# A hybrid decoder trunk on one core: rows of x scaled and transposed instead of multiplied by a diagonal, and squares added on the vector engine before they are summed

## The chip, the cores and the metric

The program runs on one core of a Trainium2 chip. The metric is the time that one execution takes on the device, in microseconds (us). PE is the matrix engine, DVE the vector engine, ACT the scalar engine, POOL the general-purpose engine; SP issues nearly all DMAs. All of them work through their own instructions in order and wait for each other by semaphores.

## The reference, cut to what matters

Two layers, each with a token mixer of four parallel groups (MLA, S5, NSA, gated DeltaNet) and a gated FFN with a short convolution. 256 tokens, 2048 features, FFN width 5632, float32. Around each of the four sub-layers stand an RMS norm before (with shift and scale computed from a conditioning vector c) and one after; three of the mixers' outputs are normalised over their 512 features, and the MLA query and key-value latents over 384 and 256.

```python
def rms_norm(x, g):
    xf = x.astype(jnp.float32)
    y = xf * lax.rsqrt(jnp.mean(xf * xf, axis=-1, keepdims=True) + NORM_EPS)
    return (y * g.astype(jnp.float32)).astype(x.dtype)

q = (rms_norm(cq, q_norm) @ w_uq).reshape(B, S, MLA_HEADS, MLA_NOPE + MLA_ROPE)
kv = (rms_norm(ckv, kv_norm) @ w_ukv).reshape(B, S, MLA_HEADS, MLA_NOPE + MLA_V)

o = jnp.concatenate([rms_norm(o_a, gn_mla), rms_norm(o_b, gn_s5), rms_norm(o_c, gn_nsa), o_d], axis=-1)
return o @ w_out
```

## The kernel before, in words

All large products are streamed: a weight tile of 128x1024 floats comes by DMA into a ring (`raw`, four buffers), ACT casts it to the high half of its mantissa (`wh`, line 366), DVE subtracts to get the low half (`wl`, line 367), and PE makes three products of halves for each pair (`mm3`, `mm` at line 127). The activations stand feature-major in the tile `ht`, in two halves too. A second stream (`rawa`, two buffers) brings the modulation weights `w_ada`; DVE multiplies and adds them into `acc` (lines 410 and 412), a tile now and then between other work.

A sub-layer begins in a **turn**. `post_block` gathers sums of squares while the last products of the sub-layer before come out (lines 575 to 586). `residual` works out the scale of the rows, sets it, and adds the new output to x, in four blocks of 512 features for each half of the tokens (line 616). `pre_norm` then makes `ht`: in steps of two chunks of 128 features (`k2`, eight steps), PE multiplies the chunk of x [128 tokens, 128 features], as the stationary operand, by a diagonal matrix `diag` of the rows' scales. This transposes and scales in one product. ACT applies the modulation's scale and shift from PSUM (line 549), DVE (first step) or ACT (the others) casts the high half (line 551), DVE subtracts the low half (line 552). The first four steps stand ahead of the weight products (`norm_start`), the others among them. The additions to x go in two groups: two blocks right behind the diagonals, two behind the first chunks' operands.

`norm_T` (line 695) normalises over features of a feature-major output: ACT squares (line 702), PE multiplies each 128x128 of squares by a column of ones and accumulates over all of them in one PSUM tile, DVE makes the reciprocal root (`row_rs`, lines 516 and 149 to 155), PE spreads it over the partitions, and DVE multiplies (line 709). It is called five times a layer: for four chunks of 256 columns by S5, MLA and NSA, for three by the MLA queries and for two by the MLA keys and values.

Transposes elsewhere go through `tp` (line 131). The order of each engine's instructions is set by a scheduler while the program is built, from the program order and from priorities: the weight stream stands up to 2500 steps ahead (`BOOST`), the turn ahead of that (`first`), and `after` puts instructions behind a given one.

Of the kernel before, what the change touches and what calls it, by code (L numbers as in the profile page):

```python
# [21 lines left out]
P = 128  # L22
# [21 lines left out]
RSC = -8192.0        # factor that rsqrt_cols leaves on its result  # L44

MBOOST = 300        # the same of the mixers' own weights
BOOST = 2500        # how far ahead of the arithmetic the weight stream is scheduled

# arena map (floats per partition)
A_KVT = 0                           # token-major narrow columns  # L50
A_SIL0 = A_KVT + 1704               # GDN inputs of heads 0, 1
A_GA = A_SIL0 + 1536                # S5, then GDN heads 0, 1, then MLA
A_SIL1 = A_GA + 6160                # S5 tables; GDN inputs of heads 2, 3
A_GB = A_SIL1 + 1536                # S5 tables; GDN heads 2, 3, then NSA
A_OT = A_GB + 7168                  # mixer outputs, feature-major
A_KEEP = A_OT + 4096                # compressed keys and values of the NSA group
NA = A_KEEP + 1024
A_X = A_KVT                         # the residual stream, but for the time of the mixers
A_Z = A_X + 4096                    # output of the mixing block before its norm
A_GP = A_SIL1                       # the output gate of the mixing block  # L60
FIRST = (O_U, O_U + 256, O_GQ)      # columns of the first products
A_TAB = A_SIL1                      # S5 tables, the rotations last
A_ROT = A_TAB + 4608
A_SCR, N_SCR = A_OT + 2048, 3072    # S5 tables being built
A_GPF = A_SCR                       # the output gate of the FFN
AT = [A_ROT + g * 1024 for g in range(4)] + [A_Z + g * 1024 for g in range(5)] + [A_OT, A_OT + 1024]   # the FFN's inner activations
ADA_DVE = (0, 2, 4, 6, 9, 11)       # tiles of a quarter that DVE multiplies
# [6 lines left out]
class Region:  # L74
    """Sequential carving of a range of the arena."""
# [16 lines left out]
class Ker:  # L92
    def __init__(self, ctx, tc, I, out):
# [5 lines left out]
        # operands in two parts of half the mantissa: h^T; then the mixer outputs, or the FFN's activations  # L99
# [410 lines left out]
    def first(self):  # L510
        """Ahead of the weight stream."""
        return self.tc.high_priority(BOOST + 1500)

# [15 lines left out]
    def pre_norm(self, l, which):  # L529
        """Fills h^T, 4 tiles of 4 chunks each; a generator that stops after each quarter of the features."""  # L530
        nc = self.nc
        for k2 in range(KT // 2):
            if k2 in (2, 4, 6):
                yield
# [1193 lines left out]
```

## Time and profile before

| | |
|---|---|
| Time of three runs | 2695.22 us median (2687.34 to 2700.55) |
| Profiled execution | span 2692.3 us from its first to its last instruction; the page gives no time of its own around it |
| Busy | PE 2553.3 us (95%), PE weight loads 2257.8 (84%), DVE 1924.8 (71%), ACT 1260.7 (47%) |
| DMA | 621.43 MB, 231 GB/s in the mean |
| Granted PE clock, mean | 0.978 |

A profile shows for each engine when an instruction was at work and what it waited for before. The stages lie like this: up to about 172 us the start (constants, the first modulation vectors, the first norm), to 560 us the mixers of the first layer, to 625 their output projection, then the first FFN to about 1418, the second layer's mixers from 1440 to 1850, their projection to 1915, and the second FFN to the end. The turns lie at 625 to 641, 1425 to 1440 and 1915 to 1930 us.

### The profile page before, as it was taken

What the parts mean: (1) busy time and instruction counts of PE and PEld (TensorE: products, weight loads), DVE (VectorE), ACT (ScalarE), POOL (GpSimd) and SP (SyncE); (2) the same over time, 40 slices, a digit from 0 to 9 for tenths busy, and PEclk for the clock granted to TensorE, in tenths of its full rate; (3) what the DMA queues carried; (4) which work ended last, traced back from release to release, by engine and by line L of the source; (5) the groups of instructions that cost most, each with busy time, mean ns of one, the idle gap of its engine ahead of it and who ended that gap; (6) DMA issues with size and microseconds to landing.
All of it is one profiled execution on the core that took longest, in us unless ns stands there. A gap on an engine that the chain in (4) does not pass through costs nothing. (4 is left out here: it accounts for less than half of the span.)

```text
span 2692.3 us, 44696 instructions
## 1 busy us (share of the span) xinstructions
PE 2553.3 (95%) x17587; PEld 2257.8 (84%) x17587; DVE 1924.8 (71%) x3036; ACT 1260.7 (47%) x2025; POOL 9.6 (0%) x21
## 2 busy tenths in 40 slices
PE   5899999798999999999998999999899999999998
PEld 2478788687999999988877879888799999998886
DVE  6668888778877777776878888865677655555555
ACT  4244554546545444444545445555544444444443
POOL 0000000000000000000000000000000000000000
PEclk7889999899999999999999999999999999999999
DMA  8986887676888888877776667835588766665554
GB/s 269 298 242 188 259 277 226 202 268 217 274 287 277 283 286 284 293 247 234 232 255 228 189 201 243 267 123 170 180 272 280 224 187 188 183 186 188 188 188 148
DMA packets 325899, 621.43 MB, mean 231 GB/s; under 512 B 45132, under 2 KB 131640, under 8 KB 324152
## 3 DMA queue, kind: packets, MB, share of 16 engines
q1 hardware_dynamic: 317632, 617.36, 71.5%
q8 instruction: 138, 2.26, 0.3%
q10 hardware_dynamic: 8056, 1.21, 0.3%
q14 instruction: 73, 0.60, 0.1%
HBM read 614.26 MB, written 4.23 MB: 230 GB/s over the span
## 5 line engine op out<-in xcount | busy, mean ns | idle before, releaser
L127 PE MATMUL mm<-ht,wh 128*128 128x256 f32 x7232 | 1311.4, 283 | 2.9 <-ACT wh L366 2.9
L366 ACT CAST wh<-raw 128x1024 fp32r<-128x1024 f32 (+1 forms) x740 | 771.2, 1043 | 953.8 <-PE mm L127 751.2
L367 DVE TENSOR_TENSOR wl<-raw,wh 128x1024 fp32r<-128x1024 f32 (+1 forms) x740 | 893.2, 1213 | 346.1 <-ACT wh L366 344.2
L127 PEld LDWEIGHTS mm<-ht,wh 128*128 128x128 f32 x7232 | 1114.1, 189 | 15.2 <-issue 6.8
L127 PE MATMUL mm<-ht,wl 128*128 128x256 f32 x3616 | 1023.9, 283 | 7.9 <-DVE wl L367 7.6
L127 PEld LDWEIGHTS mm<-ht,wl 128*128 128x128 f32 x3616 | 681.7, 189 | 20.2 <-DVE wl L367 12.8
L412 DVE SCALAR_TENSOR_TENSOR acc<-rawa,condc,acc 128x1024 f32<-128x1024 f32 x310 | 397.3, 1282 | 216.5 <-DMA rawa<-in_w_ada_dram 215.0
L127 PE MATMUL mm<-wh,ht 128*128 128x512 f32 (+1 forms) x1600 | 507.4, 395 | 3.4 <-ACT ht L366 2.9
L127 PEld LDWEIGHTS mm<-wh,ht 128*128 128x128 f32 x1600 | 300.9, 189 | 68.0 <-ACT ht L366 3.2
L127 PE MATMUL mm<-wl,ht 128*128 128x512 f32 (+1 forms) x800 | 316.1, 395 | 1.7 <-DVE wl L367 1.7
L127 PE MATMUL mx<-wh,ht 128*128 128x512 f32 x704 | 221.4, 395 | 0.0
L127 PE MATMUL mx<-arena 128*128 128x128 f32 (+8 forms) x1432 | 199.1, 280 | 12.5 <-ACT arena L1417 4.7
L127 PEld LDWEIGHTS mx<-arena 128*128 128x128 f32 (+5 forms) x1432 | 156.0, 170 | 51.4 <-issue 20.2
L127 PEld LDWEIGHTS mm<-wl,ht 128*128 128x128 f32 x800 | 151.6, 190 | 34.0 <-DVE wl L367 3.0
L127 PEld LDWEIGHTS mx<-wh,ht 128*128 128x128 f32 x704 | 132.0, 187 | 32.1
L127 PE MATMUL mx<-wl,ht 128*128 128x512 f32 x352 | 139.3, 396 | 0.9 <-DVE wl L367 0.8
L131 PE MATMUL mx<-ident,arena 128*128 128x128 f32 (+3 forms) x367 | 68.4, 290 | 32.4 <-ACT arena L1280 11.0
L367 DVE TENSOR_TENSOR ht<-arena,ht 128x1024 fp32r<-128x1024 f32 x52 | 63.6, 1223 | 39.4 <-ACT ht L366 39.0
L131 PEld LDWEIGHTS mx<-ident,arena 128*128 128x128 f32 (+3 forms) x367 | 44.4, 148 | 53.7 <-ACT arena L1280 12.7
L1557 DVE SCALAR_TENSOR_TENSOR arena<-mm,v,arena 128x255 f32<-128x255 f32 (+1 forms) x176 | 78.2, 476 | 4.3 <-ACT arena L1555 3.5
L127 PEld LDWEIGHTS mx<-wl,ht 128*128 128x128 f32 x352 | 66.0, 187 | 18.1 <-DVE wl L367 2.1
L366 ACT CAST ht<-arena 128x1024 fp32r<-128x1024 f32 x52 | 54.2, 1050 | 56.5 <-PE mm L127 32.3
(308 smaller groups left out, 1514.1 us busy)
## 6 DMA issues: line engine op xcount, KB each, us to landing
raw<-in_ffn_w_in_dram SPq DMA_DIRECT2D x352, 512.0 KB
rawa<-in_w_ada_dram SPq DMA_DIRECT2D x348, 512.0 KB
raw<-in_ffn_w_out_dram SPq DMA_DIRECT2D x176, 512.0 KB
raw<-in_w_in_dram SPq DMA_DIRECT2D x116, 512.0 KB
raw<-in_w_out_dram SPq DMA_DIRECT2D x64, 512.0 KB
rawm<-in_w_ada_dram SPq DMA_DIRECT2D x28, 512.0 KB
raw<-in_w_in_dram SPq DMA_DIRECT2D x16, 426.0 KB
raw<-in_w_in_dram SPq DMA_DIRECT2D x16, 354.0 KB
```

What stands on the lines that cost most here:

```text
L127: self.nc.tensor.matmul(out, lhsT=lhsT, rhs=rhs, start=start, stop=stop)
L131: self.nc.tensor.transpose(out, in_, self.ident[:k, :k])
L366: self.nc.scalar.copy(hi.bitcast(F32R), src)
L367: self.nc.vector.tensor_sub(lo.bitcast(F32R), src, hi)
L412: self.last_mac = self.nc.vector.scalar_tensor_tensor(acc, w, self.condc[:, kc:kc + 1], acc, op0=ALU.mult, op1=ALU.add)
L1557: nc.vector.scalar_tensor_tensor(c[:, s:], ps[m][:, :256 - s], self.fconv(l, 2 - s, f), c[:, s:], op0=ALU.mult, op1=ALU.add)
```

## The change

The diagonal is gone. `set_scale` leaves the rows' scale as two columns. `pre_norm` copies a quarter of x (512 features, both halves of the tokens) times that scale into a free place of the arena: DVE does so for the first quarter, ACT for the other three. PE then transposes the copies with `tp`. The additions to x now go in three groups: one block behind the scale, one behind the scaled copies of the first quarter, two as before. `norm_T` squares all chunks into one place of 1024 floats, DVE adds the squares down to 256 columns, and PE makes two products with the column of ones instead of two for each chunk. (Comments of the file are left out in the changed kernel; its line numbers differ a little.)

```diff
-        self.diag = t([P, 2, P], F32, "diag")
...
-    def set_diag(self, ss):
+    def set_scale(self, ss):
+
         r = self.rsqrt_cols(ss)
-        for tt in range(2):
-            i = self.nc.vector.tensor_scalar(self.diag[:, tt], self.ident, r[:, tt:tt + 1], 1.0 / RSC,
-                                             op0=ALU.mult, op1=ALU.mult)
-        return i
+        self.rs = self.sm(2, "rs")
+        return self.nc.vector.tensor_scalar(self.rs, r, 1.0 / RSC, None, op0=ALU.mult)
 
     def pre_norm(self, l, which):
         nc = self.nc
+        slots = (AT[0:4] if which else (AT[7], AT[8], AT[4], AT[5]) if l else (AT[9], AT[10]))
         for k2 in range(KT // 2):
             if k2 in (2, 4, 6):
                 yield
+            if k2 % 2 == 0:
+                q = k2 // 2
+                xs = self.reg(slots[q % len(slots)], 1024)(2, 512)
+                for tt in range(2):
+                    src = self.x[:, tt, q * 512:(q + 1) * 512]
+                    if q:
+                        nc.scalar.activation(xs[:, tt], src, AF.Identity, scale=self.rs[:, tt:tt + 1])
+                    else:
+                        i = nc.vector.tensor_scalar(xs[:, tt], src, self.rs[:, tt:tt + 1], None, op0=ALU.mult)
+                if q == 0 and self.add_rest is not None:
+                    self.add_rest[0](i)
             ps = self.mx()
             for i in range(2):
-                k = 2 * k2 + i
+                k = (2 * k2 + i) % 4
                 for tt in range(2):
-                    self.mm(ps[:, i * 256 + tt * P:i * 256 + (tt + 1) * P], self.x[:, tt, k * P:(k + 1) * P],
-                            self.diag[:, tt], True, True)
+                    self.tp(ps[:, i * 256 + tt * P:i * 256 + (tt + 1) * P], xs[:, tt, k * P:(k + 1) * P])
...
-                self.add_rest(i)
+                self.add_rest[1](i)
...
-        d = self.set_diag(t)
+        d = self.set_scale(t)
...
-        add(range(2), d)
-        self.add_rest = lambda i: add(range(2, 4), i)
+        add(range(1), d)
+        self.add_rest = [lambda i: add(range(1, 2), i), lambda i: add(range(2, 4), i)]
...
     def norm_T(self, scr, chunks, banks, n, gains, outs):
         nc = self.nc
+        o = 0
+        for b, w in banks:
+            nc.scalar.activation(scr[:, o:o + w], b, AF.Square)
+            o += w
+        sq = scr[:, 0:256]
+        if o == 1024:
+            nc.vector.tensor_tensor(scr[:, 0:512], scr[:, 0:512], scr[:, 512:1024], op=ALU.add)
+            o = 512
+        for i in range(256, o, 256):
+            nc.vector.tensor_tensor(sq, sq, scr[:, i:i + 256], op=ALU.add)
         ss = self.mx(2)
-        i, m = 0, 2 * len(chunks)
-        for bi, (b, w) in enumerate(banks):
-            sq = scr[:, bi % 2 * 512:bi % 2 * 512 + w]
-            nc.scalar.activation(sq, b, AF.Square)
-            for j in range(w // P):
-                self.mm(ss[:, j % 2:j % 2 + 1], sq[:, j * P:(j + 1) * P], self.ones[:, 0:1], i == 0, i == m - 1)
-                i += 1
+        for j in range(2):
+            self.mm(ss[:, j:j + 1], sq[:, j * P:(j + 1) * P], self.ones[:, 0:1], True, True)
```

The scheduler lays the program out anew. Three places:

PE's order at the turn into the first FFN, before (`mx` are PSUM tiles of one step each, `mm` those of the weight products):

```order
L127 MATMUL mx_5672<-diag,arena 128x128
L127 MATMUL mx_5688<-diag,arena 128x128
L127 MATMUL mx_5672<-diag,arena 128x128 x3
L127 MATMUL mx_5688<-diag,arena 128x128 x3
L127 MATMUL mx_5698<-diag,arena 128x128 x4
L127 MATMUL mx_5708<-diag,arena 128x128 x4
L127 MATMUL mm<-ht,wh 128x256 x2
```

and with the change:

```order
L131 MATMUL mx_5666<-ident,arena 128x128 x4
L131 MATMUL mx_5682<-ident,arena 128x128 x4
L131 MATMUL mx_5694<-ident,arena 128x128
L131 MATMUL mx_5704<-ident,arena 128x128
L127 MATMUL mm<-ht,wh 128x256 x3
L127 MATMUL mm<-ht,wl 128x256
L127 MATMUL mm<-ht,wh 128x256 x2
L127 MATMUL mm<-ht,wl 128x256
L127 MATMUL mm<-ht,wh 128x256
L127 MATMUL mm<-ht,wl 128x256
L127 MATMUL mm<-ht,wh 128x256 x2
L127 MATMUL mm<-ht,wl 128x256
```

Sixteen products stood ahead of the first weight product, ten transposes do now; the other six of the first four steps stand behind twelve weight products.

DVE's order at the same turn, before:

```order
L525 TENSOR_SCALAR diag<-ident,cy 128x128 x2
L616 SCALAR_TENSOR_TENSOR arena<-arena,cy 128x512 x4
L551 CAST ht<-hf 128x256
L552 TENSOR_TENSOR ht<-hf,ht 128x256
L551 CAST ht<-hf 128x256
L552 TENSOR_TENSOR ht<-hf,ht 128x256
L616 SCALAR_TENSOR_TENSOR arena<-arena,cy 128x512 x4
L552 TENSOR_TENSOR ht<-hf,ht 128x512 x2
L367 TENSOR_TENSOR wl<-raw,wh 128x1024 x2
```

and with the change:

```order
L524 TENSOR_SCALAR rs<-cy 128x2
L625 SCALAR_TENSOR_TENSOR arena<-arena,cy 128x512 x2
L542 TENSOR_SCALAR arena<-arena,rs 128x512 x2
L625 SCALAR_TENSOR_TENSOR arena<-arena,cy 128x512 x2
L560 CAST ht<-hf 128x256
L561 TENSOR_TENSOR ht<-hf,ht 128x256
L560 CAST ht<-hf 128x256
L561 TENSOR_TENSOR ht<-hf,ht 128x256
L625 SCALAR_TENSOR_TENSOR arena<-arena,cy 128x512 x4
L561 TENSOR_TENSOR ht<-hf,ht 128x512
L366 TENSOR_TENSOR wl<-raw,wh 128x1024
```

Two scalings stand between the additions of the first and second block, and one subtraction less ahead of the first split of a weight tile (`wl`).

ACT's order there with the change, from the last weight casts before the turn on (before, the two casts were followed by the shifts into `hf` at once):

```order
L365 CAST wh<-raw 128x1024 x2
L540 ACTIVATE arena<-arena,rs 128x512
L558 ACTIVATE hf<-mx_5666,mod 128x256 x2
L558 ACTIVATE hf<-mx_5682,mod 128x256 x2
L540 ACTIVATE arena<-arena,rs 128x512
L560 CAST ht<-hf 128x512
L540 ACTIVATE arena<-arena,rs 128x512
L558 ACTIVATE hf<-mx_5694,mod 128x256 x2
L540 ACTIVATE arena<-arena,rs 128x512
```

The scalings of the second and third quarter (L540) stand between the shifts and casts of the first steps.

In SP's order the loads are the same 1256 in number. Ahead of the 109th load into `raw` stood 98 loads into `rawa`, and 87 do now; ahead of the 115th it is 113 and 111, and from the 121st on to the second layer's mixers the two counts agree again.

## Rows read from the trace of the kernel before

**Rows 1.** The page, part 1: busy us, share of the span, instructions.

```profile
span 2692.3 us, 44696 instructions
PE 2553.3 (95%) x17587; PEld 2257.8 (84%) x17587; DVE 1924.8 (71%) x3036; ACT 1260.7 (47%) x2025; POOL 9.6 (0%) x21
```

**Rows 2.** By stage: length, busy us of PE, PEld, DVE, ACT, POOL, clock, DMA.

```profile
0.00:172.00 172.00, 123.04 (x676) 66.42 (x677) 104.22 (x269) 60.64 (x143) 4.61 (x13) 0.82 0.88 281
172.00:500.00 328.00, 316.72 (x2224) 271.45 (x2223) 275.48 (x546) 155.94 (x308) 0.52 (x1) 1.00 0.76 232
500.00:560.00 60.00, 47.09 (x288) 39.52 (x289) 37.49 (x80) 31.64 (x82) 2.27 (x2) 0.89 0.64 204
...
1440.00:1850.00 410.00, 400.56 (x2832) 348.29 (x2831) 317.53 (x647) 213.21 (x448) 0.52 (x1) 0.99 0.67 209
```

**Rows 3.** Timeline, turn into the first FFN: start, us, instruction, idle before and releaser.

```profile
633.25 0.48 DVE L525 TENSOR_SCALAR diag<-ident,cy 128x128 f32<-128x128 f32 x2
633.65 2.73 DVE L616 SCALAR_TENSOR_TENSOR arena<-arena,cy 128x512 f32<-128x512 f32 x4
...
634.49 6.35 PE L127 MATMUL mx<-diag,arena 128*128 128x128 f32 x32 [9.51 <-issue]
637.00 1.02 ACT L549 ACTIVATE hf<-mx,mod 128x256 f32<-128x256 f32 x2 [6.72 <-PE mx L127]
...
637.93 0.43 DVE L552 TENSOR_TENSOR ht<-hf,ht 128x256 fp32r<-128x256 f32 x1
...
640.60 0.48 PE L127 MATMUL mm<-ht,wh 128*128 128x256 f32 x2
```

**Rows 4.** Groups by line and shape, PE: count, busy us, mean ns, idle before.

```profile
L127 PE MATMUL mx<-diag,arena 128*128 128x128 f32 x256 | 40.2, 318 | 26.2 <-issue 17.9 <-DVE arena L616 7.0 <-DVE diag L525 0.7
...
L127 PE MATMUL mx<-ones,arena 128*128 128x1 f32 x168 | 20.8, 244 | 0.4 <-ACT arena L702 0.3
```

**Rows 5.** Timeline of PE: eight records of diagonal products, eight of transposes.

```profile
643.99 1.05 PE L127 MATMUL mx<-diag,arena 128*128 128x128 f32 x8
...
1633.02 1.05 PE L131 MATMUL mx<-ident,arena 128*128 128x128 f32 x8
```

**Rows 6.** Groups by line and shape, DVE.

```profile
L412 DVE SCALAR_TENSOR_TENSOR acc<-rawa,condc,acc 128x1024 f32<-128x1024 f32 x310 | 397.3, 1282 | 216.5 <-DMA rawa<-in_w_ada_dram 215.0
...
L1339 DVE TENSOR_TENSOR arena<-arena 128x512 f32<-128x512 f32 x64 | 42.0, 682 | 0.1
...
L1180 DVE TENSOR_TENSOR arena<-arena 128x256 f32<-128x256 f32 x48 | 19.5, 421 | 6.5 <-ACT arena L1242 6.0
...
L410 DVE TENSOR_SCALAR acc<-rawa,condc 128x1024 f32<-128x1024 f32 x23 | 17.2, 749 | 4.0 <-DMA rawa<-in_w_ada_dram 4.0
```

**Rows 7.** Busy time and clock around that turn; then PE's timeline near the start.

```profile
634.50:639.80 5.30, 5.30 (x25) 5.30 (x26) 4.01 (x9) 2.04 (x4) 0.00 (x0) 0.50 0.01 3
639.90:643.20 3.30, 3.30 (x31) 3.30 (x30) 3.30 (x6) 2.99 (x6) 0.00 (x0) 1.00 0.00 0
...
31.50:33.50 2.00, 1.82 (x8) 1.57 (x8) 0.85 (x7) 0.67 (x3) 0.00 (x0) 0.50 1.01 369
31.68 1.94 PE L131 MATMUL mx<-ident,arena 128*128 128x128 f32 x8 [2.80 <-DMA arena<-in_s_c_re_dram]
```

**Rows 8.** Timeline, the first layer's S5 norm.

```profile
281.52 0.16 DVE L516 TENSOR_SCALAR rv<-mx 128x2 f32<-128x2 f32 x1 [2.28 <-PE mx L127]
```

**Rows 9.** The chain that ended last, turn into the second FFN: start, us, what.

```profile
1930.95 1.21 DVE ht L552 x2
1932.16 1.15 DVE wl L367
```

**Rows 10.** Timeline, the first layer's MLA norm.

```profile
517.22 0.63 ACT L702 ACTIVATE arena<-arena 128x512 f32<-128x512 f32 x1
...
519.37 1.28 DVE L412 SCALAR_TENSOR_TENSOR acc<-rawa,condc,acc 128x1024 f32<-128x1024 f32 x1 [1.51 <-DMA rawa<-in_w_ada_dram]
520.57 0.15 DVE L516 TENSOR_SCALAR rv<-mx 128x2 f32<-128x2 f32 x1
```

More of the change, by code (lines that the diff above doesn't have):

```diff
@@ L1643, in run @@
         self.new_squares()
-        self.set_diag(self.x_stats())
+        self.set_scale(self.x_stats())
         h = self.pre_norm(0, 0)
```

## The prediction

> **What bounds the kernel now.** I read the page first: PE is busy for 95% of the span, DVE for 71%, so the first question is where PE is not kept fed [rows 1]. Busy time by stage [rows 2] puts the idle time into a few places. In the mixers of both layers PE is busy for 97% and 98% of the stage and DVE for 84% and 77%; over the last 60 us of the first layer's mixers PE falls to 78%. The other holes are the turns, where one sub-layer's output is normalised before the next one can start. There are three; I read the one into the first FFN in the timeline [rows 3]. PE stands still for 9.5 us while DVE computes the rows' scale; then DVE writes the two diagonals, adds two blocks of x, and PE starts its diagonal products at 634.49, although the first weight product comes only at 640.60, behind all 32 records of the first four chunk pairs. Its operand was ready sooner: ACT took the scaled and shifted half at 637.00, DVE cast it and subtracted at 637.93 for 0.43, so by 638.36 the operand was there. PE's own queue holds the first product back by 2.2 us.
>
> **Products against transposes.** The program has 128 products with the diagonal and the trace shows 256 records of them [rows 4]: two records each. Eight such records (four products) take 1.05 us; eight records of a transpose, which are eight transposes, also take 1.05 us [rows 5]. Less the last one's latency (0.27) that is 0.111 us for a record. So a product costs PE 0.222 and a transpose 0.111, and 128 of them give back 14.2 us of PE. A quarter of that belongs to the first norm, which lies in the opening stretch where PE is only 72% busy [rows 2]; I cost it at nothing, since loads cover it there, and at 3.6 us of loss at most if the scaling lengthens that start.
>
> **A turn, step by step** (the first FFN's, times from [rows 3]). The scale is known at 633.25. DVE then writes one tile of two columns instead of two diagonals: about 0.2 instead of 0.4. It adds the first block of x for both halves of the tokens (four take 2.73, so two about 1.4), and now scales both. A 128x512 TENSOR_SCALAR is in no row; it lies between the 128x128, two of which take 0.48 [rows 3], and the 128x1024 of 0.75 [rows 6], in proportion at about 0.47 (bounds 0.24 and 0.75). The first transposes can go at about 635.3, the second half's at 635.7: PE starts 0.8 us later than before. It is at the low level of its clock there; eight transposes in a row at that level take 1.94 us, 0.22 each [rows 7]. The four of the first chunk pair end, with latency, at about 636.8. ACT first scales half of the second block (its add ends at 636.4; a 128x512 pass of ACT takes 0.63 [rows 10], with a scale per row perhaps 0.7), so it takes the chunk at 637.1; cast and subtraction follow as before, and the first operand is there at 638.45. By the new order only ten transposes stand ahead of the first weight product, so that starts at 638.45 and not at 640.60: 2.15 us sooner. Against that, six transposes (0.65) come later among the products, and until the clock rises at 639.8 [rows 7] the products run at half speed (0.7 lost). Net gain 0.8. Chunk pairs five to eight stand among the products: 16 x 0.111 = 1.8 us less. A turn gains 2.6. One rule speaks against this; it stands with the third rival.
>
> What could take that back is the supply. ACT gets six scalings of about 0.7 per norm, 4.2 us, in a stretch in which it also shifts, casts and splits weights; DVE's four late adds and the first weight split stand in the chain of the third turn [rows 9]. There the order changes for the better: one subtraction (0.6) moves behind the first weight split. I take 7 us for three turns. Bounds: 0, if ACT's scalings hold each turn up, and 10.7, if all of the PE time of three norms (three quarters of 14.2) is gained.
>
> **Norms over features.** Ten calls lose 48 products with a column of ones, 96 records of the 168 [rows 4], 0.111 each: 10.7 us of PE. DVE gets six adds of 128x512 at 0.68 and twelve of 128x256 at 0.42 [rows 6]: 9.1 us. PE is the fuller engine in the mixers, so I count some of its time as gained, not all. On the chain of one norm it cuts both ways. In the S5 norm DVE sat idle for 2.28 us until PE had summed [rows 8]; with two adds (1.1) and two products (four records, 0.45) the sums come about 0.7 us sooner. In the MLA norm at the end of the mixers the squares were done at 517.85 but DVE was in a modulation product that had waited 1.51 us for its load; the sums were read at 520.57 [rows 10]. Adds queued behind that product would give the sums 1.6 us later. I take 3 us as the net of all ten calls; bounds are a loss of 9.1 and a gain of 10.7.
>
> **Order.** All of the mixers are laid out anew, SP's loads too: 87 modulation loads instead of 98 stand ahead of the 109th weight load, and they have caught up twelve weight loads later. Each costs DVE 1.28 us [rows 6]. It is work moved, not added: zero, with 11 x 1.28 = 14 us either way as the bound. Everything in the FFNs but the turns keeps its order.
>
> **Sum.** 7 + 3 = 10 us off the profiled execution's 2692.3 us of span. The page gives no time around that span; the median of the runs is 2695.2, 2.9 above it, and I add that: 2682.3 + 2.9 = **2685 us**.
>
> **Rivals.**
> *All PE time is gained.* PE is 97 to 98% busy in the mixers, and after a turn each record is followed by the next. Then 10.7 from the norms and 10.7 from the three turns come off: 2695.2 - 21.4 = 2674 us. Against it: DVE is at 77 to 84% there, and gets 9.1 us more.
> *Slower: DVE's queue at the end of the mixers.* DVE works in order, and it waited 215 us before its modulation products for their loads [rows 6]; every add placed behind such a product waits with it. This decides if PE runs out of weight products there, as it did between 500 and 560 [rows 2]. Price: the eleven modulation products moved towards the end at 1.28 plus the mean wait of 0.7 (215 us over their 310), 21.8 us, and 1.6 us at each of the four late norms, less the turns' 7 and a little from the early mixers, about 5: 16 us more, 2711 us. For it speaks PE's 78%; against it, that the loads moved are missing earlier, and that between the softmax steps the new order has no more of these products than the old one.
> *The clock stays low.* At the first FFN's turn PE stood still for 9.5 us [rows 3], the granted clock was 0.50 (1.2 GHz) while it did diagonal products, and 1.00 (2.4 GHz) from 639.9 [rows 7]. If transposes do not bring it back as those products did, the rise comes later by the time from the first record to the first weight product, 638.45 - 634.49 = 4.0 us, in which half the work is lost: 2.0 a turn, 6 in all, and nearly all of the turns' gain is gone: 2691 us. The eight transposes in rows 7 also ran at 0.50, but only just after a wait, so the trace does not decide. The Trainium skill, TensorE: Matmul & The Clock Gate, Part 4 (PE-mode transpose), says that the full clock "doesn't engage" for transposes; by that rule this rival holds, and no long run of transposes alone in this trace shows it.
> *It does not do what it says.* A transpose costs no less than a product once its scaled copy is counted: 32 passes of ACT and DVE (eight a norm) replace PE time that was never waited for. Then the time stays at 2695. Rows 3 speak against it, since PE's queue is what the first weight product waits for.
>
> **How the numbers follow.** Runs of this kernel lie between 2687 and 2701, so 0.5% (13.5 us) is about what can be told from no change; below 2682 is faster, above 2709 slower. Chances: forecast 0.45 (2677 to 2693), all PE time gained 0.30, low clock 0.10, no effect 0.05, slower 0.10. Faster: the second case and the lower quarter or so of the first, 0.40. Slower: 0.10. The rest, 0.50, is no change. The range runs from 2670, just under the case of all PE time with some favour of the order, to 2704, above no effect by some of the order's 14 us; it leaves out most of the slower case and the tails.
>
> **What would show it.** Right: the first weight product of the first FFN about 3.1 us after PE's first transpose of the turn, where 6.1 lay behind the first diagonal product, ten transposes ahead of it, transposes with one record each, PE's busy time down by some 20 us. Wrong in the turn: ACT's scalings end PE's waits, or the granted clock rises later than 5 us after PE resumes. Wrong in the mixers: PE's share between the MLA norm and the last norm falls below 78%, or DVE's wait for modulation loads grows well past 215 us.

## The result, and the profile after

The changed kernel takes 2709.6 us (median of 6 runs, 2700.2 to 2712.3), the kernel before 2694.0 (6 runs): a ratio of 1.0062, interval 1.0042 to 1.0082. It is **slower by 0.6%**, 15.6 us, where 2685 was forecast and 2704 was the end of the range. Four of the six runs lie at 2709 to 2712 and two at 2700 to 2701; the trace is of one of the four.

The page of the changed kernel, part 1:

```profile
span 2708.2 us, 44327 instructions
PE 2544.3 (94%) x17363; PEld 2238.9 (83%) x17363; DVE 1937.9 (72%) x3058; ACT 1278.5 (47%) x2053; POOL 9.6 (0%) x21
```

Against [rows 1], PE is busy for 9.0 us less, and yet the span grew. The groups of records that the change touches, the transposes before and after and the products with ones after, shrank by more:

```profile
L131 PE MATMUL mx<-ident,arena 128*128 128x128 f32 x334 | 63.3, 294 | 28.2 <-ACT arena L1280 11.0 <-ACT arena L740 8.3 <-DMA arena<-in_s_c_re_dram 2.8
```

```profile
L131 PE MATMUL mx<-ident,arena 128*128 128x128 f32 x462 | 87.6, 308 | 70.9 <-DVE arena L542 27.6 <-ACT arena L754 17.5 <-ACT arena L1294 11.1
L127 PE MATMUL mx<-ones,arena 128*128 128x1 f32 x72 | 9.6, 244 | 3.1 <-DVE amx L742 2.3 <-DVE arena L716 0.7
```

The 128 new transposes take 24.3 us where the diagonal products took 40.2, and the products with ones 9.6 where they took 20.8 [rows 4]. But the mean granted clock fell from 0.978 to 0.969, and at the lower level a record takes longer (eight transposes 1.94 us at 0.50 in [rows 7], 1.05 in [rows 5]).

Busy time by stage (length, then busy us of PE, PEld, DVE, ACT, POOL, clock, DMA share, GB/s) tells where:

```profile
0.00:172.00 172.00, 117.75 (x631) 59.15 (x632) 101.31 (x262) 61.40 (x141) 4.62 (x13) 0.81 0.84 274
172.00:500.00 328.00, 312.53 (x2165) 265.54 (x2163) 272.43 (x535) 159.04 (x304) 0.53 (x1) 0.99 0.74 232
500.00:560.00 60.00, 40.26 (x191) 32.80 (x190) 37.14 (x87) 28.40 (x89) 0.00 (x0) 0.72 0.48 153
```

Against [rows 2], PE falls from 47.1 to 40.3 us between 500 and 560, its clock there from 0.89 to 0.72, and the DMA share from 0.64 to 0.48. A stage cut at fixed times compares different work, though. So the first layer is cut here at three instructions that both kernels have: DVE reads the sums of S5's norm (`rv<-mx`, the first), those of the recurrence's second pair of heads (`rv<-gss`, the third), and reduces the block sums at the first turn (`bt<-bs`). Weight tiles are counted by their splits on DVE:

| stretch, us | before | before, a second trace | after |
|---|---|---|---|
| A: start to S5's sums | 281.5 (42 tiles) | 281.7 | 290.3 (43) |
| B: to the second heads' sums | 105.0 (20) | 107.9 | 116.1 (25) |
| C: to the first turn | 241.9 (45) | 242.4 | 246.8 (39) |
| first turn to second | 800.0 | 799.5 | 794.7 |
| second turn to third | 489.3 | 486.5 | 487.1 |
| third turn to the end | 774.6 | 775.5 | 773.3 |

Two traces of the kernel before differ by 3.6 us at most at these points. The change loses 8.7 + 11.1 + 4.9 = 24.7 us in the first layer up to its first turn and gains 8.8 after it: all of the loss lies in A, B and C (against the second trace, 21.1 are lost there and 5.2 gained after). Of these, B holds five more weight tiles than before, and C six fewer. A weight tile is just under 3 us of PE (in the FFN, 200 splits of the kernel before take 595 us), so B is longer by less than the work that moved into it. C, with some 18 us less to do at the full clock, should be shorter by as much; it is 4.9 longer. Stretch C, before and then after:

```profile
386.50:628.40 241.90, 218.68 (x1349) 181.99 (x1347) 187.41 (x377) 117.72 (x248) 2.27 (x2) 0.97 0.74 241
```

```profile
406.30:653.10 246.80, 209.81 (x1242) 172.70 (x1240) 181.56 (x374) 111.44 (x240) 2.28 (x2) 0.92 0.67 219
```

PE is busy there for 8.9 us less, at a mean granted clock of 0.92 and not 0.97, and stands still for 37.0 us and not 23.2.

The groups of DVE in stretch C, before and then after (busy, mean ns of one, idle time ahead):

```profile
L412 DVE SCALAR_TENSOR_TENSOR acc<-rawa,condc,acc 128x1024 f32<-128x1024 f32 x53 | 67.9, 1281 | 20.4 <-DMA rawa<-in_w_ada_dram 20.2
```

```profile
L411 DVE SCALAR_TENSOR_TENSOR acc<-rawa,condc,acc 128x1024 f32<-128x1024 f32 x51 | 65.4, 1282 | 35.5 <-DMA rawa<-in_w_ada_dram 35.3
```

About as many modulation products as before, but DVE waits 15 us longer for their loads (12.5 longer than in the second trace of before, which has 22.8). Over the whole program this wait is 215.0 and 186.3 us in the two traces of before and 196.6 after, so the sum over a program does not show it. The chain that ended last shows what this looks like, in the changed kernel from 504 us on (start, us, what):

```profile
504.40 1.20 DVE acc L411
...
505.62 4.88 DMA rawa<-in_w_ada_dram
...
510.60 1.30 DVE acc L411
511.92 4.37 DMA rawa<-in_w_ada_dram
516.31 1.29 DVE acc L411
...
517.62 4.35 DMA rawa<-in_w_ada_dram
...
522.06 1.30 DVE acc L411
523.37 4.29 DMA rawa<-in_w_ada_dram
```

A product frees its buffer, the next load into it lands 4.3 us later, and there are two buffers: two products every 5.7 us, with DVE in order and the softmax steps behind them. That is the pace when nothing else lies between. Before, weight tiles lay between: the longest row of modulation products without a split of a weight tile among them has 12 in both traces of before (496.8 to 534.7 in the first), and **23** after (470.0 to 541.3).

The turn into the first FFN, which answers to [rows 3]:

```profile
658.05 0.17 DVE L524 TENSOR_SCALAR rs<-cy 128x2 f32<-128x2 f32 x1
658.12 1.41 DVE L625 SCALAR_TENSOR_TENSOR arena<-arena,cy 128x512 f32<-128x512 f32 x2
659.45 0.87 DVE L542 TENSOR_SCALAR arena<-arena,rs 128x512 f32<-128x512 f32 x2
...
660.08 2.49 PE L131 MATMUL mx<-ident,arena 128*128 128x128 f32 x10 [10.42 <-DVE arena L542]
...
661.65 1.91 ACT L558 ACTIVATE hf<-mx,mod 128x256 f32<-128x256 f32 x4
662.23 0.29 DVE L560 CAST ht<-hf 128x256 fp32r<-128x256 f32 x1 [0.58 <-ACT hf L558]
...
662.57 1.04 PE L127 MATMUL mm<-ht,wh 128*128 128x256 f32 x3
```

The first weight product comes 2.5 us after the first transpose, ten transposes ahead of it, as forecast (6.1 and sixteen products before). From the reduction of the block sums to the 192nd weight record it takes 38.4, 37.8 and 37.7 us at the three turns before, and 35.6, 36.1 and 36.4 after: 2.8, 1.8 and 1.3 gained, 5.9 in all. The granted clock there:

```profile
664.40:664.80 0.40, 0.40 (x4) 0.40 (x3) 0.40 (x1) 0.40 (x2) 0.00 (x0) 0.53 0.00 0
664.80:665.20 0.40, 0.40 (x5) 0.40 (x5) 0.40 (x2) 0.40 (x1) 0.00 (x0) 1.00 0.00 0
```

It reaches 1.00 at 664.8, 4.7 us after PE resumed (5.3 before). And two norms, on DVE: S5's, for [rows 8], then MLA's, for [rows 10]:

```profile
285.38 1.27 DVE L411 SCALAR_TENSOR_TENSOR acc<-rawa,condc,acc 128x1024 f32<-128x1024 f32 x1
286.57 0.69 DVE L713 TENSOR_TENSOR arena<-arena 128x512 f32<-128x512 f32 x1
287.18 1.22 DVE L366 TENSOR_TENSOR wl<-raw,wh 128x1024 fp32r<-128x1024 f32 x1
288.31 0.42 DVE L716 TENSOR_TENSOR arena<-arena 128x256 f32<-128x256 f32 x1
...
290.26 0.16 DVE L515 TENSOR_SCALAR rv<-mx 128x2 f32<-128x2 f32 x1 [1.14 <-PE mx L127]
...
533.42 1.28 DVE L411 SCALAR_TENSOR_TENSOR acc<-rawa,condc,acc 128x1024 f32<-128x1024 f32 x1 [1.62 <-DMA rawa<-in_w_ada_dram]
534.62 0.68 DVE L713 TENSOR_TENSOR arena<-arena 128x512 f32<-128x512 f32 x1
535.23 0.68 DVE L741 TENSOR_REDUCE amx<-mx 128x2 f32<-128x512 f32 x1
535.83 0.42 DVE L716 TENSOR_TENSOR arena<-arena 128x256 f32<-128x256 f32 x1
...
537.00 0.16 DVE L515 TENSOR_SCALAR rv<-mx 128x2 f32<-128x2 f32 x1 [0.68 <-PE mx L127]
```

The adds stand in DVE's queue behind whatever was laid ahead of them: a split of a weight tile between S5's two adds, a modulation product that had waited for its load ahead of MLA's. From the end of the last square to the sums, six norms (S5, MLA, NSA of both layers) took 2.5, 2.7, 2.0, 2.2, 1.8 and 1.8 us before and 4.6, 2.7, 3.2, 5.3, 2.5 and 2.2 after.

### The profile page after: what moved, and what is told of

Read it like the earlier page. It is cut to its first block, busy times and chain, and to the rows that moved or that the text cites. A ratio compares the mean times of both kernels' runs of the same rounds, so it can differ in the third digit from the quotient of the medians.

```text
span 2708.2 us, 44327 instructions
## 1 busy us (share of the span) xinstructions
PE 2544.3 (94%) x17363; PEld 2238.9 (83%) x17363; DVE 1937.9 (72%) x3058; ACT 1278.5 (47%) x2053; POOL 9.6 (0%) x21
## 4 chain that ended last, share of the span: by engine, by line
PE 73%; DMA 11%; DVE 9%; ACT 3%; issue 3%; SPq 0%; ACTq 0%; DVEq 0%
PE mm L127 55%; PE mx L127 16%; DMA rawa<-in_w_ada_dram 9%; DVE wl L366 3%; DVE acc L411 2%; PE mx L131 2%; ACT wh L365 1%; DMA rawm<-in_w_ada_dram 1%; DMA raw<-in_w_in_dram 1%; ACT junk L584 1%; DMA rawm<-in_nsa_w_v_dram 0%; DMA arena<-in_s_c_im_dram 0%; DVE arena L590 0%; ACT arena L1294 0%; DVE arena L1044 0%
## 5 line engine op out<-in xcount | busy, mean ns | idle before, releaser
L411 DVE SCALAR_TENSOR_TENSOR acc<-rawa,condc,acc 128x1024 f32<-128x1024 f32 x310 | 397.3, 1282 | 197.4 <-DMA rawa<-in_w_ada_dram 196.6
L127 PE MATMUL mx<-arena 128*128 128x128 f32 (+8 forms) x1432 | 206.7, 289 | 16.7 <-DVE arena L1044 5.9
L127 PEld LDWEIGHTS mx<-arena 128*128 128x128 f32 (+5 forms) x1432 | 162.6, 177 | 62.0 <-issue 18.9
L131 PE MATMUL mx<-ident,arena 128*128 128x128 f32 (+3 forms) x495 | 92.9, 304 | 76.0 <-DVE arena L542 27.6
L131 PEld LDWEIGHTS mx<-ident,arena 128*128 128x128 f32 (+3 forms) x495 | 63.5, 155 | 100.4 <-issue 33.7
```

Source lines behind the costliest of these rows:

```text
L127: self.nc.tensor.matmul(out, lhsT=lhsT, rhs=rhs, start=start, stop=stop)
L131: self.nc.tensor.transpose(out, in_, self.ident[:k, :k])
L411: self.last_mac = self.nc.vector.scalar_tensor_tensor(acc, w, self.condc[:, kc:kc + 1], acc, op0=ALU.mult, op1=ALU.add)
```

## The experiments

Three theories were tried. *Operations*: the adds, scalings and transposes cost it. *Modulation queue*: DVE stands behind modulation loads at the end of the first mixers. *Order of the weight products*: the scheduler, given other operations, lays the weight products further ahead; they delay the recurrence's steps on PE and are missing at the end (first put as "no filler", then as "ahead of the chain"). Each ratio is to runs of the kernel before on the same chip. A trace is one run and need not lie at the median: e5's took 2708.8 us, e7's 2688.0 and e13's 2693.2, where the medians are 2702.1, 2680.0 and 2699.4.

**Each half alone.** e1 is the changed kernel with the function `norm_T` of before, e2 the kernel before with the new one:

```
 e1, against the change
-        for j in range(2):
-            self.mm(ss[:, j:j + 1], sq[:, j * P:(j + 1) * P], self.ones[:, 0:1], True, True)
...
+            for j in range(w // P):
+                self.mm(ss[:, j % 2:j % 2 + 1], sq[:, j * P:(j + 1) * P], self.ones[:, 0:1], i == 0, i == m - 1)
...
```

> The scaled and transposed rows alone; the norms over features as before. In this order the weight products stand only about one tile (2.6 us of PE) further ahead of the recurrence's steps than before, and 97 modulation loads (98 before) stand ahead of the 109th weight load. If the loss comes from the order in the first layer's mixers, in either form below, nearly nothing of it is here and the turns' gain of 1 to 2 us each is seen: 2688 to 2697 us against 2694 before. If the transposes at the low clock, or the scalings on ACT and DVE, cost the loss: 2703 to 2710.

> The norms over features alone; the products with the diagonal as before. If the order of the first layer's mixers is the cause: this order brings the weight products two to four tiles further ahead of the recurrence and 88 modulation loads instead of 98 ahead of the 109th weight load, so nearly all the loss is here: 2705 to 2715 us. If the adds themselves cost it (18 passes of DVE, 9.1 us, less 10.7 us of PE): no more than 2703. If the turns are the cause: 2694.

e1: 2708.0 us, 1.0051 (1.0031 to 1.0071). e2: 2712.5, 1.0066 (1.0046 to 1.0086). Each half costs as much as the whole, in different places: e1 reaches the first turn only 3.8 us later than before, and loses 15 between the second and third turn; e2 loses 17.8 before the first turn and nothing after the second. Two parts that each cost the whole are not two prices that add up. The forecast for e1 failed: I had looked at the order of the first layer alone.

**Weight products held back at the end.** In the changed kernel, as edges between instructions of PE (e3; in e4 the pair is 24, 34):

```
-            ps = self.gemm_b(W, O_GZ + hp * 256)
+            with self.after(self.marks[(8, 20)[hp]]):
+                ps = self.gemm_b(W, O_GZ + hp * 256)
```

`marks` are the last products of the recurrence's steps, 20 for each pair of heads.

> The changed kernel, with the products of the GDN output gate (8 weight tiles, 21 us of PE) held behind two steps of the GDN recurrence on PE, so that about as many weight products are left for the end of the first mixers as before the change; the modulation products of that end stay there (12 between the first and the last softmax step, 14 with the change). Theory 'no filler' (PE has used up its weight products before the latency-bound end): 5 to 15 us of the loss come back, 2695 to 2705 us. Theory 'modulation queue' (DVE stands behind late modulation loads in that end): 2709, as with the change.

> The same, the products of the output gate held further back: by the order some 11 weight tiles (29 us of PE) are left at the end of the GDN recurrence, where the change leaves none and the kernel before two. Theory 'no filler': at least all of the loss comes back, 2680 to 2697 us. Theory 'modulation queue': 2709 give or take 5.

e3: 2711.8 us, 1.0058 (1.0037 to 1.0080). e4: 2712.0, 1.0063 (1.0043 to 1.0082). Nothing came back, so "no filler" as put there falls. PE stood at the holds instead: in e4 it is busy for 33.9 of the 50 us from 400 on, at a clock of 0.69. The longest bare row of modulation products is 11 in both, and yet C takes 248.0 us in e3 and 242.1 in e4.

**All weight tiles of the mixers held to their old places.** Each tile's products get PE edges to the steps that stood ahead of them before (a table of 94 tiles a layer):

```
-        self.mm(out, a[0], b[0], start, False)
...
+        keys = zip(("s5", "nsa_compress", "gdn_half", "gdn_half", "mla", "nsa"), PIN.get(self.nw, ()))
+        with self.after(*[self.marks[k] for k in keys if k in self.marks]):
+            self.mm(out, a[0], b[0], start, False)
...
```

> The changed kernel, with every weight tile's products in the first layer's mixers put on PE behind the same step of S5, the recurrence, MLA and NSA as before the change (no more than one tile off anywhere; with the change they run up to six tiles, 16 us of PE, ahead at the recurrence). The modulation products of DVE keep the places that the change gave them (37 loads used at the recurrence's first step where before had 33; 79 to 93 between the first and the last softmax step). Theory 'weight products ahead of the chain' (the steps of S5 and the recurrence wait on PE behind weight products, which are then missing at the end): the 22 us lost in the first mixers come back, and with the 4 us gained at the second layer's turn and in its mixers it ends at 2686 to 2696 us. Theory 'modulation queue': 2705 to 2712. Theory 'the operations themselves': 2705 to 2712.

> The same pinning in both layers' mixers. The second layer's mixers lose nothing with the change (19 us behind at their start, 16 at their end), so by 'weight products ahead of the chain' they can gain up to 5 us more or nothing: 2683 to 2696 us; by the other two theories 2705 to 2712.

e5: 2702.1 us, 1.0027 (1.0012 to 1.0042): half came back. B is 107.2 us with 21 tiles. But PE waits at the pins for an S5 that is late (293.0; PE is busy for 46.0 of the 50 us from 250 on, 49.7 before), and C stays at 247, with a longest bare row of 9. e6: 2709.3, 1.0060 (1.0039 to 1.0081): pins in the second layer cost there. A pin gives the place, not the readiness.

**Modulation tiles left out**, in the changed kernel (e7) and in the one before (e8):

```
+        w = None
...
-            self.ada_mac(acc, self.ada_tile(l, b, kc, 1), kc, kc == 0)
+            if l or b not in (6, 9) or w is None:
+                w = self.ada_tile(l, b, kc, 1)
+                self.ada_mac(acc, w, kc, kc == 0)
```

> The changed kernel with 30 of the first layer's modulation tiles left out (two blocks of the FFN's shift and scale use one tile of weights of 16, so those vectors are not computed); all 12 or so loads and products between the first and the last softmax step of the first mixers are gone, and the order of weight products against the steps is as with the change to within one tile. Theory 'modulation queue' (DVE stands behind late modulation loads at that end): the end gains at least the 12 products and their waits, 12 x (1.28 + 0.64) = 23 us, so 2680 to 2690 us. Theory 'weight products ahead of the chain': the lateness of 12 to 20 us at the recurrence stays and the end has no more work to fill PE: 2700 to 2709 us.

> The kernel before with the same 30 modulation tiles of the first layer left out (those shift and scale vectors are not computed). The changed kernel without them took 2680 us, 30 less than with them. If the change loses by what these loads and products do at the end of the first mixers, the kernel before gains less from their absence, and the two end within 5 us of each other: 2676 to 2686. If they stand in the way of both kernels alike, the 15.6 us between the two stay: 2660 to 2668.

e7: 2680.0 us, 0.9939 (0.9922 to 0.9957). e8: 2674.2, 0.9921 (0.9904 to 0.9939). A and B of e7 are as late as with the change (second heads' sums 19.6 us behind before), then C takes 221.0 us instead of 246.8. In C of the kernel before, 241.9 became 224.1. So these loads and products limit C in both kernels; and without them the change costs 0.18% by the two ratios (each good to about 0.18%), not 0.62%, so much of its loss seems to need them. Whether the products or the traffic of their loads do it, these two runs do not tell. The forecast that the two would end within 5 us was just missed (5.8).

**The first norm.** e9 is e5 with the program's first norm by 32 diagonal products as before, e11 the changed kernel with that alone, e10 the kernel before itself. `pre_norm_diag` is the `pre_norm` of before:

```
-        self.set_scale(self.x_stats())
-        h = self.pre_norm(0, 0)
+        self.set_diag(self.x_stats())
+        h = self.pre_norm_diag(0, 0)
```

> As the pinned kernel of the first layer (2702 us, 7.6 less than the change), and the first norm of the program with its 32 diagonal products as before; the three turns and the ten norms over features are as changed. If the 8 us that are left come from the opening stretch, where the pinned kernel's S5 norm was 11.5 us late, they go too: 2690 to 2697 us. If the opening differs between runs anyway, 2698 to 2706.

> The kernel before once more, for a second trace: how far do the times of one and the same step differ between two executions? If the opening's loads set them, the tenth weight split (152.9 us in the first trace, 157 to 166 in the traces of all the others) comes at 150 to 156 again where the order is what costs, and at 157 or later where it is chance.

> The changed kernel with the first norm of the program as before (32 diagonal products), nothing pinned. 'The opening costs': S5's norm comes at 280 to 285 us again (281.5 before, 290.2 with the change), and 5 to 9 us of the 15.6 come back: 2700 to 2705 us. By its order the weight products stand one to four tiles ahead of the recurrence (five to six with the change), so the stretch from S5's norm to the recurrence's second head group should be 3 to 9 us longer than before. 'The opening is chance': 2706 to 2712.

e9: 2696.9 us, 1.0005 (0.9989 to 1.0021), no loss left; its interval and that of e5 overlap, so the first norm's share of the return is not clear of noise. Its trace has A back (281.3), but B takes 116.3 us with only 20 tiles: PE stands still for 10.6 us of it (3.7 before), and its clock is 0.94 where it was 1.00 before. So the number of tiles is not all that sets B. e10 gave the second column of the table of stretches; the split that the forecast calls the tenth (counted from zero) came at 155.4, where the order and not chance would have it. e11: 2712.2, 1.0050 (1.0034 to 1.0066): S5's sums come at 285.7, but B takes 120.0 us with 24 tiles, and C has 22 modulation products in a row. The eight traces with the old first norm have S5's sums at 280.1 to 285.7, the eleven with the new one at 284.4 to 295.2: the opening is later by it, mostly by 5 to 10 us, but alone it decides nothing.

**Other engines and places for the modulation.** e12 has the products of two blocks on GpSimd, in the changed kernel:

```
+            if l == 0 and b in (6, 9):
+                c = self.condc[:, kc:kc + 1].to_broadcast([P, 1024])
+                self.nc.gpsimd.tensor_tensor(w if kc else acc, w, c, op=ALU.mult)
+                if kc:
+                    self.nc.gpsimd.tensor_tensor(acc, acc, w, op=ALU.add)
```

> The changed kernel with two of the six modulation blocks of the first layer (the 32 tiles whose products fall into the end of its mixers) multiplied and added on GpSimd, two passes of 128x1024 a tile, instead of one pass on DVE; nothing else changed. No row of these traces gives the length of such a pass. 'Modulation queue on DVE': DVE no longer stands behind these loads, and as without the tiles (2680) most of the 15.6 us and more come back, 2682 to 2698 us, if a tile takes GpSimd less than about 6 us; if it takes longer, the turn into the first FFN waits for the last tile and it is slower than the change: 2712 to 2760.

2764.2 us, 1.0236 (1.0214 to 1.0259). In e12 the two passes of a tile are:

```profile
L428 POOL TENSOR_TENSOR acc<-acc,rawa 128x1024 f32<-128x1024 f32 x30 | 74.3, 2478 | 2.3
L426 POOL TENSOR_TENSOR rawa<-rawa,condc 128x1024 f32<-128x1024 f32 x30 | 59.7, 1989 | 90.0 <-DMA raw<-in_w_out_dram 73.8 <-DMA rawa<-in_w_ada_dram 16.2
```

4.5 us a tile and long waits: the first turn is 52 us later than with the change. The forecast for less than 6 us a tile was a gain, so it failed: the passes were short enough, and POOL's waits (90.0 us ahead of the first of the two) had been left out. e15 to e17 keep the products on DVE and move them out of MLA and NSA:

```
-        bg = ((((0, (4, 5, 8, 6, 9, 7)),), (0.5, 0.6, 1, 0.8)), ...
+        bg = ((((0, (4, 5, 8, 6, 9, 7)),), (0.5, 0.6, 0, 1.4)), ...
+        self.bg_rate = 0.0 if l == 0 else self.bg_rate
```

The last line stands ahead of MLA's first weight products; e15 is the changed kernel, e16 has the lookahead of e13 (below) as well, e17 is the kernel before.

> The changed kernel; in the first layer no modulation tile is put between the products of MLA and of NSA (6 loads between the first and the last softmax step by the order, 14 with the change), and the output projection takes 1.4 for each weight tile instead of 0.8. The opening and the recurrence keep the change's order. Theory 'modulation queue at the end': from the recurrence's second heads to the turn it takes some 8 x (1.28 + 0.64) = 15 us less than the change's 246.7, less up to 5 us for the fuller projection: 2694 to 2702 us. If DVE's queue is not what limits that end: 2706 to 2714.

> The same with the lookahead of 600, by which the weight products stand nearly as before at the recurrence (2699 us with that alone). Theory 'modulation queue at the end': 7 to 15 us less than 2699: 2684 to 2692 us, faster than both kernels. Otherwise 2696 to 2704.

> The kernel before with the same move of modulation tiles out of MLA and NSA. Theory 'modulation queue at the end': this end of the kernel before has the queue too (17.1 us of waits for its loads between 440 and 620), so it gains as well, though less: 2684 to 2692 us. Otherwise 2692 to 2698.

All are slower, against the forecast: 2718.4 (1.0084, 1.0069 to 1.0099), 2707.0 (1.0048, 1.0030 to 1.0067) and 2727.5 (1.0117, 1.0098 to 1.0136). Yet C did what the theory said: 222.1 in e15 (246.8 with the change), 231.5 in e16 (246.8 in e13), 232.6 in e17 (241.9). The gain was lost behind the turn, where the FFN's shift and scale were not ready: the longest bare row of e15, 15 products, runs there (644.8 to 684.9). In e15, from 642 to 690:

```profile
642.00:690.00 48.00, 12.90 (x93) 12.18 (x92) 27.84 (x27) 10.71 (x19) 0.00 (x0) 0.61 0.62 186
```

PE is busy for 13 of 48 us. The projection did not take up the products that MLA and NSA had lost: 94, 96 and 96 modulation products stand ahead of the first turn in the three traces, where 109 stand there in before, after and e13, so 13 to 15 were left for after the turn. That stood in the order ahead of the runs; I had counted only up to the last softmax step. No version here that computes everything is clearly faster than the kernel before.

**Order alone, both ways.** e13 is the changed kernel with the first of these edits, e14 the kernel before with the second:

```
-MBOOST = 300
+MBOOST = 600
...
-(0.5, 0.6, 1, 0.8)
+(0.55, 0.6, 1, 0.8)
```

> The changed kernel with one number changed: the lookahead of the mixers' own small weights, 300 to 600. All operations are the change's. By its order the weight products stand where the kernel before had them (52 tiles ahead of the recurrence's eighth step where before had 52 and the change 57; 73 ahead of the 49th where before had 72 and the change 76). Theory 'order': the stretch from S5's norm to the recurrence's second heads takes 105 to 109 us (105 to 108 before, 116 with the change); the opening stays as late as with the change; 5 to 12 us come back: 2697 to 2704 us. Theory 'operations': 2706 to 2712.

> The kernel before with one number changed: 0.55 modulation tiles for each weight tile in the first mixers instead of 0.5. No operation is changed; the scheduler lays the mixers anew, with the weight products two to four tiles (5 to 10 us of PE) further ahead of the recurrence and gone by the end of its second half. Theory 'order': 5 to 12 us slower than before, 2699 to 2707 us. Theory 'operations': 2692 to 2697, no change.

e13: 2699.4 us, 1.0013 (0.9995 to 1.0031). All of the change's operations are in it, and some 10 of the 15.6 us came back. B takes 106.0 us with 22 tiles, and A stays late (288.6). But C did not come back:

```profile
394.60:641.50 246.90, 216.15 (x1292) 177.76 (x1290) 187.70 (x379) 114.82 (x244) 2.27 (x2) 0.94 0.72 231
```

It is as long as with the change (246.8), though it holds 43 weight tiles, though the longest bare row of modulation products is 9 and not 23, and though DVE waits 26.2 us for their loads and not 35.3. So the row alone does not set the length of C. In this trace the first turn still comes 13.1 us later than before, and the work behind it takes that back (789.8 us from the first turn to the second, 800.0 before). The number holds for the second layer's mixers too, but the stretch from the second turn to the third stays as with the change (487.5 and 487.1). e14: 2694.4, 0.9996 (0.9977 to 1.0014), no loss where one was forecast: B grew to 112.1 with 22 tiles, and C (42 tiles) shrank to 235.2, with the bare row at 12 and the wait at 21.1. Weight products brought forward cost nothing here, since C shrank by nearly as much as B grew.

## Why the prediction was wrong

**The turns**: right. 7 us forecast, 5.9 measured; ten transposes ahead, one record each. The first product came 4.5 us behind the scale, 5.2 forecast: it started as soon as the cast of its operand's high half was done (662.23 for 0.29), while the prediction had it wait for the subtraction too. The rivals that spoke against it fall: ACT's scalings (724 ns) end none of PE's waits there, and the clock rises early. The Trainium skill, TensorE: Matmul & The Clock Gate, Part 4 (PE-mode transpose), has it that the full clock "doesn't engage" for transposes. Here it came 2.2 us behind the first weight product, and no later after PE resumed than with the diagonal products, so ten transposes ahead did not hold it back. No run here has a longer stretch of transposes alone, so the rule itself stays untested. (The price of that rival mixed two kernels: its 4.0 us run from the old kernel's first record to the new one's first product; by the prediction's own start of 635.3 they are 3.1.) PE's busy time was to fall by some 20 us and fell by 9.0, while its mean clock fell from 0.978 to 0.969.

**The norms**: the count was right (168 records to 72, 20.8 us to 9.6; adds of 0.69 and 0.42), the sign on the chain wrong. "The sums come about 0.7 us sooner" in S5 became 2.1 later, since DVE's first add and its second had other work ahead of them in the queue. The six norms above give their sums 7.6 us later in all, where 3 us of gain were put down for ten.

**The opening**, "I cost it at nothing ... 3.6 us of loss at most": S5's sums came 8.7 us later.

**Order** is the step that failed: "It is work moved, not added: zero, with 11 x 1.28 = 14 us either way as the bound". I counted modulation loads against weight loads (87 and not 98 ahead of the 109th) and read it as modulation put off, caught up twelve weight loads later. By SP's order in the two traces, 110 loads into `rawa` stand ahead of the 110th load into `raw` in both kernels: the eleven were not spread over twelve weight loads but stand in one row, 23 loads between two weight loads where there were 12. Counted against the steps of the mixers, as many modulation products as before stand in each stretch (29 and 29 in B, 55 and 53 in C); it was the weight products that had moved, five tiles into B. B grew by 11.1 us, and C, with six tiles fewer, did not shrink but grew by 4.9. e13 shows the size: the same operations in another order took 2699.4 us, with B 1.0 us longer than before. e11 and e9 are a second pair with the same operations, and differ in the pins alone: 1.0050 without them and 1.0005 with them, with intervals that do not meet. So about 10 of the 15.6 us belong to the order and are no fixed price of the operations. The rest is not clear of noise in e13 (1.0013, 0.9995 to 1.0031). The forecast gain of 10 us came in neither order: the later S5 sums and the longer C stay in e13, and the gain of the turns goes into covering them.

**The slower rival**, at 0.10, gave 2711 us and named the place: DVE in order behind modulation loads at the end of the first mixers. DVE does wait longer there, but neither of the signs set for it came. Between the MLA norm and the last norm PE is busy for 30.7 of 35.5 us (537.0 to 572.5), 86%, where it was 24.7 of 30.5, 81% (520.6 to 551.1); the 67% between 500 and 560 belongs, with the change, mostly to what lies ahead of the MLA norm. And the wait over the program stayed under 215. Its sum (eleven moved products at 1.28 + 0.7) was not what happened either, so that it nearly hit the time is chance.

**Open.** Which of the new operations makes the scheduler bring the weight products forward was not tried, and neither was the kernel before with e13's lookahead of 600: if that gained as well, the operations would cost more than e13 alone says. e1's 15 us in the second layer have another cause, not found: its longest row there is 6 products, before 7. And C of the kernels with the new norms is 241 to 249 us with all tiles in place, of those with the old ones 235 to 242. That speaks for a price of the new norms themselves in C, by the adds in DVE's queue or by what they move; no run parts the two.

## What to carry to other kernels

Where a scheduler lays the work, a change of a few operations is a change of the order of everything near them, and that can be worth more than the operations (here 10 us against a forecast gain of 10): count what moved against the steps of the dependent chain, not against another stream that may itself have moved. Work brought forward is free only if the stretch that it leaves gets shorter; see what limits that stretch before you count on it. A long bare row of a stream that is paced by a small ring marks a place to look at, but it is not a price: rows of 9, 11 and 23 products went with a C of 246.8, 248.0 and 246.8 us. And price an edit by a second layout of the same operations (here one number, 15.6 us down to 4.7) before judging the operations by one, and give the kernel before that layout too.

## Not expected of the hardware

A load of 512 KB into a free buffer landed 4.3 us later in the bare row, with the DMA engines 64% busy there (504 to 528 us; 94% between 320 and 340, where they moved 302 GB/s): the next load started only when a product had freed one of the two buffers. A pass of 128x1024 on GpSimd took 1.99 to 2.48 us, where DVE does product and sum in one of 1.28. A 128x512 TENSOR_SCALAR took 0.48 on DVE, as bounded.
